# A hybrid decoder block in fp32 on one core: every third low part of the weights, from the 70th tile on, subtracted by GpSimd and not by VectorE

## The chip, the core and the metric

The kernel runs on one core of a Trainium2 chip. A core has TensorE (PE in the profile; its weight loads are PEld), VectorE (DVE), ScalarE (ACT), GpSimd (POOL) and SyncE (SP), each with an instruction queue of its own that is worked off in order, and 16 DMA engines. The metric is the time of one execution of the whole program on the device, in microseconds (us).

## The reference

One decoder block for a sequence of 256 tokens of width 2048, in float32:

```python
mod = jax.nn.silu(c) @ w_ada[l] + b_ada[l]
sh1, sc1, g1, sh2, sc2, g2 = jnp.split(mod, 6, axis=-1)
h = modulate(rms_norm(x, norm1_g[l]), sh1, sc1)
proj = h @ w_in[l]                                  # 2048 -> 6144
...                                                 # attention heads and gated short convolutions
x = x + g1[:, None, :] * (mixed @ w_out[l])         # 2048 -> 2048
h2 = modulate(rms_norm(x, norm2_g[l]), sh2, sc2)
u = causal_dwconv(h2 @ w_ffn_up[l], ffn_conv_w[l], ffn_conv_b[l])   # 2048 -> 11264
u_gate, u_up = jnp.split(u, 2, axis=-1)
ffn = (jax.nn.silu(u_gate) * u_up) @ w_ffn_down[l]  # 5632 -> 2048
x = x + g2[:, None, :] * ffn
```

All weights are read once; there is one sequence, so every weight matrix meets only 256 tokens.

## The kernel before

The matrix products run on TensorE in the type fp32r, and each float32 operand is carried as two fp32r numbers: a high part, the operand rounded to fp32r, and a low part, the operand less its high part. A product is the sum of three: high by high, high by low and low by high.

The weights of the four large products (`w_in`, `w_out`, `w_ffn_up`, `w_ffn_down`) come in 202 pieces, called slots in the code and numbered from 0. A piece holds four blocks (in the last product also three or two) of 128 rows by 512 columns, so it is a tile `raw` of 128 partitions by 2048 elements (1536, 1024). Slots 0 to 47 are `w_in`, 48 to 63 `w_out`. From slot 64 on come the feed-forward layers in four segments, each first through `w_ffn_up` and then through the rows of `w_ffn_down` that belong to it: up 64 to 95, down 96 to 111, up 112 to 131, down 132 to 143, up 144 to 163, down 164 to 175, up 176 to 191, down 192 to 201.

Every piece passes through these steps:

- `load_next` (line 228) issues the piece's DMA on SP's queue (lines 247 and 252) into one of 6 `raw` buffers. The rows of `w_ada`, with which the conditioning vector is multiplied, share this queue and these buffers (line 300).
- `split_hi` (line 260) has ACT round the piece into a tile `hi` (line 266). For two pieces of the last product DVE first multiplies the piece by a gate (line 264).
- `split_lo` (line 269) has DVE subtract `hi` from `raw` into a tile `lo` (line 272). Both inputs lie in SBUF. When this and the rounding are done the `raw` buffer is free, and `load_next` is called for the next transfer.
- The slot's matmuls use `hi` and `lo`: lines 866 (high) and 869 (low) in `w_ffn_up`, line 852 in its first 8 slots, lines 432 (low), 434 and 435 (high) in the other products.

There are 3 buffers each of `hi` and `lo`.

The order of the instructions on every engine is written by hand: the pool is under `manual_schedule`, and the loop of lines 1336 to 1360 walks over the slots. In the turn of slot i it emits the split of slot i + 2, then or before it the small tasks that a table has put there, then the matmuls of slot i, then the work of the `w_ada` tiles that are due in that slot. So a piece's low part is emitted two slots ahead of its use, and a slot takes TensorE 4 to 6 us.

DVE's other work in the feed-forward part: the multiply-adds of `w_ada` (line 330, elements by a column of the conditioning vector, summed in place), the sums of partial products out of PSUM (line 762), the two taps of the convolution (line 730), the product of the gate and up halves (line 781) and its low part (line 784), and the layer's scaled and shifted input `h2` (lines 682 and 687 for two chunks of it, 695 and 707 for others). At the end lines 813, 814 and 811 scale and add the results.

GpSimd has constants and a few small DMAs at the start, and twice the start of a wide `w_ada` sum (`Ada.home`, lines 304 to 310): a memset of 128 by 2048 elements and a DMA of 8 KB on its own queue. Its second pair is emitted at slot 100's split.

Of the kernel before, what the change touches and what calls it, by code (L numbers as in the profile page):

```python
# [8 lines left out]
F32 = mybir.dt.float32  # L9
F32R = mybir.dt.float32r  # L10
AF = mybir.ActivationFunctionType
ALU = mybir.AluOpType
# [16 lines left out]

CFG = {'ada': [[0, 12, 512, False, 17, 4], [4, 8, 512, False, 66, 9], [0, 4, 512, True, 4, 6],
# [102 lines left out]
def tile_block(  # L135
# [5 lines left out]
    nc = tc.nc  # L141
    mm = nc.tensor.matmul
    act = nc.scalar.activation
    V = nc.vector
# [8 lines left out]

    N_T2K, N_T1K, N_RAW, N_HL, N_T4K = CFG["bufs"]

# [72 lines left out]
    def load_next():  # L228
        if pending:
            if isinstance(pending[0], Ada):  # L230

                pending.pop(0).home()
                return
            t = sb.tile([P, 4, 512], F32, tag="raw", bufs=N_RAW, name="raw")
            pending.pop(0)(t)
            ready.append(t)
# [23 lines left out]
    def split_hi(nk, gate=None):  # L260
# [5 lines left out]
        act(hi[:, :nk], t[:, :nk], AF.Copy)  # L266
        halfway.append((t, hi, nk))

    def split_lo():
        t, hi, nk = halfway.pop(0)  # L270
        lo = sb.tile([P, 4, 512], F32R, tag="lo", bufs=N_HL, name="lo")
        V.tensor_tensor(out=lo[:, :nk], in0=t[:, :nk], in1=hi[:, :nk].bitcast(F32), op=ALU.subtract)  # L272
        splits.append((hi, lo))
        load_next()

# [123 lines left out]
    def at(i, f, *a):  # L399
        tasks.setdefault(i, []).append((CFG["cls"].get(f.__name__, 0), f, a))  # L400

# [62 lines left out]
    turns, upto = [], {}  # L464
    for f, ka, kb in CFG["turns"]:
        fs, step = ((f,), 4) if f in COL else ((f + "0", f + "1"), 2)
# [9 lines left out]
    for i, (fs, k) in enumerate(turns):  # L476
        def near(f, d):
            u = uses[f]
            n = u.index(i) + d
            return 0 <= n < len(u) and abs(u[n] - i) <= CFG["keep"].get(f, CFG["near"])  # L480

# [107 lines left out]
    for n, (f, part, k) in enumerate(seq):  # L589
# [7 lines left out]
        if f < 3 and k == 4:  # L597
            at(i + CFG["hold"][f], hold_a, f)
        elif f < 3 and k == 12:
            at(i + CFG["evac"][f], evac_out, f)  # L600
            at(i + CFG["sq"][f], sq_out, f)
# [678 lines left out]
    hi, lo = (sb.tile([P, 4, 512], F32R, tag=g, bufs=N_HL, name=g) for g in ("hi", "lo"))  # L1280
# [26 lines left out]
    xn_copy(6, 7)  # L1307
    split_hi(slots[1][1])
    split_lo()

    vecs = []
# [24 lines left out]
    for i in range(len(slots)):  # L1336
        more = i + LA < len(slots)
        hi_late = i == N_OUT or i in CFG["hi_late"]
        last = i in CFG["x_first"]
        if more and not hi_late and not last:  # L1340
            split_hi(slots[i + LA][1], gated.get(i + LA))
        now[0] = i
        todo = sorted(tasks.pop(i, []), key=lambda e: e[0])
        for c, f, a in todo:
            if c < 2:
                f(*a)
        if more and hi_late and not last:
            split_hi(slots[i + LA][1], gated.get(i + LA))
        if more and not last:
            split_lo()  # L1350
        for c, f, a in todo:
            if c == 2:
                f(*a)
        hi, lo = splits.pop(0)
        slots[i][2](hi, lo)
        for g, r in extra.get(i, []):
            g.consume(r)
        if more and last:
            split_hi(slots[i + LA][1], gated.get(i + LA))
            split_lo()  # L1360
# [33 lines left out]
```

## Time and profile before

| | |
|---|---|
| time, median of 3 runs | 1169.39 us (1168.94 to 1169.49) |
| profiled execution: span from its first to its last instruction | 1167.8 us |
| median of the runs less this span | 1.6 us |
| TensorE's granted clock over the span | 1.000 |
| low parts (line 272) | 201, of them 130 from slot 72 on |
| DMA, mean over the span | 272 GB/s |

The profile is one execution. It states its span and no time of its own beside it; the 1.6 us are what the unprofiled runs take longer than the span of the profiled one, and stand for what lies around the program's instructions. "Idle before" in a row is the time in which the engine did nothing just ahead of the instruction, and the arrow names the work whose end released it. In a view over stretches of time, "busy" is the time in the stretch in which the engine worked. A group's "mean ns" is the mean duration of one instruction.

### The profile page before, as it was taken

Reading aid. Unit: us, or ns where it says so; the run is one execution under the profiler, and the core shown is the slowest. Engines: PE = TensorE matmul, PEld = TensorE weight load, DVE = VectorE, ACT = ScalarE, POOL = GpSimd, SP = SyncE. Lnnn points to the kernel's source line nnn. Section 1 sums busy time; section 2 is a strip of 40 time slices with the busy share of each in tenths; the row PEclk is TensorE's granted clock in tenths of the full one; section 3 lists DMA queues with packets and bytes.
Section 4 is the critical chain, followed back from the end, with each engine's and each line's share of the span. In section 5 each row is a group of like instructions: output and inputs, shape, how many; then the busy total and the mean of one; then the engine's idle time right before and its main releaser. Section 6 shows DMA issues by size and latency. Waiting matters only on the chain.

```text
span 1167.8 us, 15668 instructions
## 1 busy us (share of the span) xinstructions
PE 1150.5 (99%) x6115; PEld 973.7 (83%) x6115; DVE 922.0 (79%) x1030; ACT 625.9 (54%) x906; POOL 12.0 (1%) x24
## 2 busy tenths in 40 slices
PE   5999999999999999999999999999999999999998
PEld 3777778888887889988888888888888888888887
DVE  3889989999999978899976767986655576577767
ACT  5645365567785565566664434455435455335451
POOL 1000000000000000000000000000000000000000
PEclk9999999999999999999999999999999999999999
DMA  9999989999899799974555897984564555675451
GB/s 361 406 415 406 409 323 362 390 346 346 288 346 338 251 319 337 364 258 166 185 202 183 304 342 277 315 290 160 198 227 156 198 181 195 225 247 181 145 180 73
DMA packets 189051, 318.00 MB, mean 272 GB/s; under 512 B 7072, under 2 KB 105844, under 8 KB 184624
## 3 DMA queue, kind: packets, MB, share of 16 engines
q1 hardware_dynamic: 187232, 314.60, 75.5%
q10 hardware_dynamic: 1296, 2.16, 0.5%
q8 instruction: 48, 0.79, 0.3%
q0 software_dynamic: 448, 0.24, 0.1%
q14 instruction: 27, 0.22, 0.0%
HBM read 312.77 MB, written 4.19 MB: 271 GB/s over the span
## 4 chain that ended last, share of the span: by engine, by line
PE 91%; DMA 3%; DVE 3%; ACT 2%; issue 0%; SPq 0%; ACTq 0%
PE z L866 24%; PE z L869 12%; PE z L852 3%; PE ada L324 1%; PE mk L434 1%; PE mk L435 1%; PE mk L432 1%; PE mq L434 1%; DVE lo L272 1%; PE mq L435 1%; PE mq L432 1%; DVE ada L330 1%; PE mc L434 1%; PE mx L434 1%; PE mx L435 1%; PE mc L435 1%
## 5 line engine op out<-in xcount | busy, mean ns | idle before, releaser
L272 DVE TENSOR_TENSOR lo<-raw,hi 128x2048 fp32r<-128x2048 f32 (+2 forms) x201 | 445.9, 2224 | 139.2 <-ACT hi L266 120.7
L266 ACT ACTIVATE hi<-raw 128x2048 fp32r<-128x2048 f32 (+2 forms) x201 | 373.6, 1865 | 311.9 <-PE z L866 58.5
L866 PE MATMUL z<-h,hi 128*128 128x512 f32 x1280 | 299.0, 390 | 0.2 <-DVE h L687 0.2
L866 PEld LDWEIGHTS z<-h,hi 128*128 128x128 f32 x1280 | 237.5, 188 | 48.2 <-PE z L866 0.6
L330 DVE SCALAR_TENSOR_TENSOR ada<-raw,csil,ada 128x512 f32<-128x512 f32 (+3 forms) x167 | 195.4, 1175 | 5.7 <-DMA raw<-in_w_ada_dram 2.2
L869 PEld LDWEIGHTS z<-h,lo 128*128 128x128 f32 x1280 | 159.3, 191 | 3.4
L869 PE MATMUL z<-h,lo 128*128 128x256 f32 x1280 | 160.5, 283 | 0.0
L730 DVE SCALAR_TENSOR_TENSOR uy<-ub,fc,uy 128x254 f32<-128x254 f32 (+1 forms) x176 | 71.3, 476 | 0.2
L762 DVE TENSOR_TENSOR ub<-z,ub 128x256 f32<-128x256 f32 x96 | 33.9, 416 | 37.9 <-ACT ub L759 37.9
L783 ACT ACTIVATE gh<-uy 128x512 fp32r<-128x512 f32 x22 | 13.9, 632 | 63.2 <-DVE uy L781 63.2
L852 PE MATMUL z<-h,hi 128*128 128x256 f32 x256 | 46.6, 284 | 0.4 <-ACT h L684 0.2
L725 ACT ACTIVATE uy<-ub,fc,fc 128x256 f32<-128x256 f32 x88 | 45.6, 602 | 0.0
L759 ACT ACTIVATE ub<-z 128x256 f32<-128x256 f32 x96 | 28.8, 384 | 31.4 <-PE z L866 31.4
L852 PEld LDWEIGHTS z<-h,hi 128*128 128x128 f32 x256 | 40.0, 192 | 0.8 <-ACT h L684 0.5
L852 PE MATMUL z<-h,lo 128*128 128x256 f32 x128 | 36.2, 283 | 0.0
L324 PE MATMUL ada<-raw,crep 128*32 128x256 f32 (+1 forms) x192 | 20.3, 534 | 7.9 <-DMA raw<-in_w_ada_dram 7.9
L784 DVE TENSOR_TENSOR gl<-uy,gh 128x512 fp32r<-128x512 f32 x22 | 15.2, 693 | 15.4 <-ACT gh L783 15.4
L434 PE MATMUL mq<-hi,h 128*128 128x512 f32 x64 | 25.5, 398 | 0.4 <-DVE adaz L361 0.4
L434 PE MATMUL mx<-hi,h 128*128 128x512 f32 x64 | 25.7, 401 | 0.0
L434 PE MATMUL mc<-hi,h 128*128 128x512 f32 x64 | 25.6, 400 | 0.0
L434 PE MATMUL mk<-hi,h 128*128 128x512 f32 x64 | 25.1, 393 | 0.0
L434 PE MATMUL mv<-hi,h 128*128 128x512 f32 x64 | 25.1, 392 | 0.0
(612 smaller groups left out, 1881.2 us busy)
## 6 DMA issues: line engine op xcount, KB each, us to landing
raw<-in_w_ada_dram SPq DMA_DIRECT2D x96, 1024.0 KB, 6.7
raw<-in_w_ffn_up_dram SPq DMA_DIRECT2D x176, 512.0 KB, 4.4
raw<-in_w_in_dram SPq DMA_DIRECT2D x47, 1024.0 KB, 7.6
raw<-in_w_ffn_down_dram SPq DMA_DIRECT2D x28, 1024.0 KB, 5.0
raw<-in_w_out_dram SPq DMA_DIRECT2D x16, 1024.0 KB, 5.4
raw<-in_w_ffn_down_dram SPq DMA_DIRECT2D x20, 768.0 KB, 4.2
xr<-in_x_dram SPq DMA_DIRECT2D x2, 1024.0 KB, 6.7
x<-in_x_dram SPq DMA_DIRECT2D x8, 256.0 KB, 6.9
```

The costliest lines, as they stand in the source:

```text
L266: act(hi[:, :nk], t[:, :nk], AF.Copy)
L272: V.tensor_tensor(out=lo[:, :nk], in0=t[:, :nk], in1=hi[:, :nk].bitcast(F32), op=ALU.subtract)
L324: mm(self.acc[q:q + 32, :], crep[:, i, :], t[:, j, :], start=(r == 0 and j < 4), stop=(r == self.tiles - 1 and j >= self.rows - 4), tile_p ...
L330: V.scalar_tensor_tensor(out=self.acc, in0=t[:, j, :], scalar=csil[:, i:i + 1], in1=self.acc, op0=ALU.mult, op1=ALU.add)
L434: mm(o, a, hi[:, k, s], start=(first and k == 0), stop=False)
L435: mm(o, b, hi[:, k, s], start=False, stop=False)
L725: act(y[:, s], b[:, s], AF.Identity, bias=bias[:, i + j:i + j + 1], scale=w[2][:, i + j:i + j + 1])
L730: V.scalar_tensor_tensor(out=o[:, d:], in0=v[:, :256 - d], scalar=w[2 - d][:, i + j:i + j + 1], in1=o[:, d:], op0=ALU.mult, op1=ALU.add)
L762: V.tensor_tensor(out=d, in0=zp[grp][ft][:, :256], in1=d, op=ALU.add)
L852: mm(o, w[:, j, a], h2T[k + j][:, v * 256:v * 256 + 256], start=begins and j == 0 and w is hi and not v, stop=ends and j == 3 and w is lo)
L866: mm(zp[grp][ft], hi[:, j, ft * P:(ft + 1) * P], h2T[k + j], start=begins and j == 0, stop=ends and j == 3)
L869: mm(zp[grp][ft][:, :256], lo[:, j, ft * P:(ft + 1) * P], h2T[k + j][:, :256], start=False, stop=False)
```

## The change

A counter numbers the calls of `split_lo`. The first call is that of slot 1 (slot 0 is split by hand), so the number is the slot's. From number 70 on, every number that 3 divides has its subtraction issued on GpSimd's queue; all others stay on DVE. Those are slots 72, 75, 78 and so on to 201, 44 pieces in all.

```diff
+CFG = {'other': [70, 3],
...
+    split_no = [0]
+
     def split_lo():
         t, hi, nk = halfway.pop(0)
         lo = sb.tile([P, 4, 512], F32R, tag="lo", bufs=N_HL, name="lo")
-        V.tensor_tensor(out=lo[:, :nk], in0=t[:, :nk], in1=hi[:, :nk].bitcast(F32), op=ALU.subtract)
+        split_no[0] += 1
+        other = split_no[0] >= CFG["other"][0] and split_no[0] % CFG["other"][1] == 0
+        (nc.gpsimd if other else V).tensor_tensor(out=lo[:, :nk], in0=t[:, :nk], in1=hi[:, :nk].bitcast(F32),
+                                                  op=ALU.subtract)
         splits.append((hi, lo))
         load_next()
```

Tiles, sizes, buffers, the order in which the instructions are emitted, and the other engines' work stay as they are.

More of the change, by code (lines that the diff above doesn't have):

```diff
@@ L28 @@
 SH1, SC1, G1, SH2, SC2, G2 = range(6)
-CFG = {'ada': [[0, 12, 512, False, 17, 4], [4, 8, 512, False, 66, 9], [0, 4, 512, True, 4, 6],
+CFG = {'other': [70, 3],
+ 'ada': [[0, 12, 512, False, 17, 4], [4, 8, 512, False, 66, 9], [0, 4, 512, True, 4, 6],
          [4, 0, 1024, False, 23, 22], [0, 8, 512, True, 11, 12], [0, 2, 256, True, 0, 5],
```

## Prediction

> **What bounds the kernel.** I read the page first, then who waited for whom, then the busy time by stretch, then single places in order of time.
>
> ```profile
> PE 1150.5 (99%) x6115; PEld 973.7 (83%) x6115; DVE 922.0 (79%) x1030; ACT 625.9 (54%) x906; POOL 12.0 (1%) x24
> ...
> PE 91%; DMA 3%; DVE 3%; ACT 2%; issue 0%; SPq 0%; ACTq 0%
> ...
> L272 DVE TENSOR_TENSOR lo<-raw,hi 128x2048 fp32r<-128x2048 f32 (+2 forms) x201 | 445.9, 2224 | 139.2 <-ACT hi L266 120.7
> ```
>
> TensorE is busy 99% of the span and is 91% of the chain that ended last. The low parts are DVE's largest group, but DVE has idle time. All waits of PE:
>
> ```profile
> PE ada L324 <- DMA raw<-in_w_ada_dram: 7.9, 3, 7.1
> PE pv_ccol L201 <- DMA vcb<-in_c_dram: 4.6, 1, 4.6
> PE mq L434 <- DVE adaz L361: 0.4, 1, 0.4
> PE mg L496 <- ACT h L1297: 0.4, 1, 0.4
> PE z L852 <- ACT h L684: 0.2, 1, 0.2
> PE z L866 <- DVE h L687: 0.2, 1, 0.2
> ```
>
> Columns: sum, times, longest, in us. The first moved piece, slot 72, is subtracted at 467 us (below). From there on only the last row's 0.2 us is a wait of PE's matmuls. So a faster DVE can win next to nothing, and the change can lose only where a low part, or DVE work behind it, becomes late by more than its slack. Whether there is slack depends on the stretch:
>
> ```profile
> 464.20:488.29 24.09, 24.09 (x175) 22.74 (x174) 23.04 (x24) 12.01 (x23) 0.00 (x0) 1.00 1.05 364
> 505.64:557.55 51.91, 51.91 (x299) 45.88 (x298) 47.20 (x72) 32.77 (x49) 0.00 (x0) 1.00 0.63 213
> 728.80:765.82 37.02, 37.02 (x210) 32.58 (x209) 34.24 (x35) 16.62 (x18) 0.00 (x0) 1.00 0.93 319
> ```
>
> The columns are the stretch, its length, busy time of PE, PEld, DVE, ACT and POOL, then PE's clock, DMA share and GB/s. PE is busy without a gap, and DVE is idle for only 24.09 - 23.04 = 1.05, 51.91 - 47.20 = 4.71 and 37.02 - 34.24 = 2.78 us. These are the places where a disturbance of DVE is felt. The n-th instruction of line 272 belongs to slot n, so slots are found by counting.
>
> **What is removed.** 44 subtractions leave DVE's queue, up to 2.29 us each (2048 elements); issued back to back they advance it by 2.24 (the pair of 4.49 us below). DVE also loses the wait for ACT's `hi` ahead of them. Worth to the end: the 0.2 us above, and as much as 0.3 at the last slot, by the list of who waited for line 272:
>
> ```profile
>   PEld m('D', 3, 3)0_9720 L432: 0.3, 1
> ```
>
> **What is added: the duration.** The trace has no GpSimd instruction with two inputs. The nearest rows:
>
> ```profile
> 174.98 1.82 POOL L308 MEMSET ada<- 128x2048 f32 x1 [79.11 <-DVE ada L330]
> ```
> ```profile
> 172.80 0.75 DVE L328 TENSOR_SCALAR ada<-raw,csil 128x1024 f32<-128x1024 f32 x1
> 173.58 1.29 DVE L330 SCALAR_TENSOR_TENSOR ada<-raw,csil,ada 128x1024 f32<-128x1024 f32 x1
> 174.79 4.49 DVE L272 TENSOR_TENSOR lo<-raw,hi 128x2048 fp32r<-128x2048 f32 x2
> ```
>
> POOL writes 2048 elements per partition in 1.82 us. If it passes the two inputs one after the other at that pace, with the write beside them, a piece costs 3.64; with all three in a row 5.46; the floor is 1.82. I take T = 4.53, half way between 3.64 and 5.46, an estimate. The Trainium skill (GPSIMD Engine Reference, 3.1) gives a measured 4497 ns for this operation at 2048 fp32 elements against 2293 on VectorE; DVE's row agrees (2.29), POOL's no run shows, and by it the sum below would be 0.3 us smaller.
>
> **What is added: the effect on DVE.** The decisive unknown is whether POOL can read two inputs while DVE reads two. Bounds: side by side costs DVE nothing, and strict turns cost it T for each piece, less the 2.24 it no longer spends. In the rows above the memset lies beside the pair of subtractions, which are not stretched, so a POOL write disturbs nothing; that is no reading. Two rows lean to turns. DVE passes 1024 elements in 0.75 us with one input (line 328) and in 1.29 with two (line 330): a one-input operation gets the second read path's help, so a two-input operation fills both. And once a POOL instruction that reads lies beside a DVE one:
>
> ```profile
> 1.01 0.29 POOL masks.py:199 TENSOR_SCALAR_AFFINE_SELECT ident<-ident 128x128 f32<-128x128 f32 x1
> ```
> ```profile
> 1.03 0.35 DVE L188 CAST onesr<-ones 128x128 fp32r<-128x128 f32 x1
> 1.93 0.23 DVE L194 CAST maskb<-mask 128x128 bf16<-128x128 f32 x1 [0.54 <-POOL mask L191]
> ```
>
> That cast took 0.35 us against 0.23 for a cast of the same size later, to another type: weak, but on the same side. I take turns, so a moved piece costs DVE 4.53 - 2.24 = 2.29 us more than before. A page speaks against this change outright: the Trainium skill (SBUF — State Buffer, Who interferes with whom) says that a VectorE instruction with two SBUF inputs contends with a GpSimd instruction that reads SBUF, and that whichever comes second is blocked until the first is done. No run here shows it; by it the sum is the one that I take, without it the first rival's.
>
> Nearly all of DVE's work here has two SBUF inputs (lines 330, 730, 781, 784, 767 and the remaining 272); line 762, out of PSUM, has one and passes. Now the places.
>
> **Place 1, slot 76.**
>
> ```profile
> 467.07 2.29 DVE L272 TENSOR_TENSOR lo<-raw,hi 128x2048 fp32r<-128x2048 f32 x1 [0.58 <-ACT hi L266]
> ...
> 486.08 2.29 DVE L272 TENSOR_TENSOR lo<-raw,hi 128x2048 fp32r<-128x2048 f32 x1
> 488.29 1.41 DVE L762 TENSOR_TENSOR ub<-z,ub 128x256 f32<-128x256 f32 x4
> ...
> 499.46 0.48 DVE L687 SCALAR_TENSOR_TENSOR h<-h2f,B,h 128x256 fp32r<-128x256 f32 x1 [0.18 <-ACT h L684]
> ```
> ```profile
> 500.09 3.89 PE L866 MATMUL z<-h,hi 128*128 128x512 f32 x16 [0.18 <-DVE h L687]
> ```
>
> The first two rows are slots 72 and 75. PE at 500.09 waits for the `h2` of line 687, which comes at the end of a chain of DVE and ACT steps that begins at 488.29. No slack: two moved pieces are 4.58 late, less the 1.05 idle of the stretch, 3.5 us.
>
> **Place 2, slot 87.**
>
> ```profile
> 557.55 2.29 DVE L272 TENSOR_TENSOR lo<-raw,hi 128x2048 fp32r<-128x2048 f32 x1
> ```
> ```profile
> 559.16 4.01 PEld L869 LDWEIGHTS z<-h,lo 128*128 128x128 f32 x32
> ```
>
> The 32 loads are the last 16 of slot 86 and the first 16 of slot 87 (a slot that ends a sum begins with its low products, line 863), which thus needs its low part at 559.16 + 2.0 = 561.2; it had it at 559.84, slack 1.3. Of DVE's 4.71 us idle since 505.64, 2.1 are three waits for ACT between lines 781 and 784 that move along with the work:
>
> ```profile
> L784 DVE TENSOR_TENSOR gl<-uy,gh 128x512 fp32r<-128x512 f32 x3 | 2.1, 692 | 2.1 <-ACT gh L783 2.1
> ```
>
> 2.6 can be filled. Slots 78, 81 and 84 make DVE 3 x 2.29 = 6.9 late, less 2.6, 4.3; ACT's `hi` of slot 87 stands behind that same chain. Its own subtraction is 4.53 - 2.29 = 2.2 longer: 4.3 + 2.2 - 1.3 = 5.2 us.
>
> **Place 3, slot 125.**
>
> ```profile
> 765.82 2.29 DVE L272 TENSOR_TENSOR lo<-raw,hi 128x2048 fp32r<-128x2048 f32 x1
> ```
> ```profile
> 768.45 4.01 PEld L869 LDWEIGHTS z<-h,lo 128*128 128x128 f32 x32
> ```
>
> Needed at 768.45 + 2.0 = 770.45, there at 768.11: slack 2.3. Since 728.80 DVE's idle time consists of hand-backs from ACT that move along, and slots 120 and 123 make it 4.6 late: 2.3 us.
>
> **Place 4, the last slot, 201.**
>
> ```profile
> 1153.65 2.28 DVE L264 TENSOR_TENSOR raw<-raw,ada 128x2048 f32<-128x2048 f32 x1
> 1158.00 2.29 DVE L272 TENSOR_TENSOR lo<-raw,hi 128x2048 fp32r<-128x2048 f32 x1 [2.06 <-ACT hi L266]
> ```
> ```profile
> 1160.34 0.98 PE L432 MATMUL m('D', 3, 3)0_9720<-lo,gh 128*128 128x512 f32 x3
> ```
>
> PE uses this low part the moment it is there, so 2.2 us more are 2.2 us later, unless the gate multiplication at 1153.65 moves ahead: two moved pieces before it (195, 198) leave DVE, 4 us at most. Between 0 and 2.2; I take 1.0.
>
> Elsewhere I find no slot whose slack is used up by the moved pieces since DVE's last gap, and count nothing. Queues: POOL has only these subtractions, and one memset and DMA after slot 100's split, which wait for that slot's work on DVE and for no moved piece; the next moved piece is two slots later. On SP the load that takes a moved piece's `raw` buffer waits up to 2.2 us longer (4.5 under turns), and the transfers queued behind it wait too.
>
> **The sum.** 3.5 + 5.2 + 2.3 + 1.0 = 12.0 on the profiled span of 1167.8 makes 1179.8; the median of the runs is 1.6 above that span: 1181.4 us. With T = 3.64 a piece costs 1.40 more: 2.8 - 1.05 = 1.75; 4.2 - 2.6 + 1.35 - 1.3 = 1.65; 2.8 - 2.3 = 0.5; end 0: 3.9, so 1173.3. With T = 5.46 (3.22 more): 5.4; 9.7 - 2.6 + 3.2 - 1.3 = 9.0; 4.1; end 2: 20.5, so 1189.9.
>
> **Rivals.** *Side by side* (the other side: not slower). POOL reads while DVE reads, and no place pays. DVE is 2.24 earlier for each piece ahead of slots 76, 87 and 125; slot 87's 4.53 - 2.29 - 1.3 = 0.9 is covered by slot 84's departure, and slot 201 by those of 195 and 198. Time 1169.4, at best 0.5 less. It decides as soon as a piece takes less than about 2.8 us from DVE: then place 1's 2 x (2.8 - 2.24) is within its 1.05 of idle time. For it: the unstretched pair beside the memset. Against: the two rows above. *Starved*: DVE keeps its reads as long as it has work, and POOL waits for a gap. From 469.36, where slot 72's subtraction ended, to 486.08 there is next to none, so it would run from 486.08 to 490.6, and slot 72 needs it here:
>
> ```profile
> 480.22 2.08 PE L869 MATMUL z<-h,lo 128*128 128x256 f32 x16
> ```
>
> That is 10.4 us late, three times place 1; with half that excess at the other places about twice the sum, 1193. For it: nothing in the trace; against: an engine that gets each turn at the end of an instruction needs no gap. *Faster*: only from those 0.5 us and a shorter tail.
>
> **Chances.** Turns 0.58, of which 0.02 end within 0.2% (2.3 us, about what a measurement of this kernel can tell from no change); starved 0.08; side by side 0.31, of which 0.28 are within 0.2% and 0.03 slower, where T is at its upper end and the last slot pays; faster 0.03. So slower 0.56 + 0.08 + 0.03 = 0.67, same 0.30, faster 0.03. The likeliest case's own range is 1173 to 1190; since side by side holds 0.31 the range reaches to it: 1168.8 to 1190.
>
> **What would show it.** Right: POOL busy some 190 us in 44 instructions of line 277; DVE two-input instructions of unchanged shape that last longer, or stand idle with POOL as releaser or with none, while POOL runs; PE waits at lines 687, 869 and 432 of 2 to 5 us near 500, 561 and 770 us. Wrong: the remaining DVE subtractions keep 2.29 us with POOL running beside them and PE has no wait, or a POOL piece lasts beyond 5.5 us with DVE undisturbed.

## The result and the profile after

| | before | after |
|---|---|---|
| time, median (range) | 1169.16 us (1168.93 to 1169.49) | 1181.21 us (1180.29 to 1182.67), 4 runs |
| profiled execution: span | 1167.8 us | 1178.5 us (that run's own time 1180.29 us) |
| ratio of the times, 95% interval | | 1.0103 [1.0091, 1.0116] |

The change costs 12.05 us; the forecast was 1181.4 us. In the program after, `split_lo` is line 277; every line of before behind it has its old number plus 6 (330 is 336, 687 is 693, 866 is 872).

First the engines and the chain that ended last, from the page of after:

```profile
PE 1152.1 (98%) x6115; PEld 974.6 (83%) x6115; DVE 923.5 (78%) x986; ACT 625.1 (53%) x906; POOL 219.1 (19%) x68
...
PE 86%; DVE 5%; DMA 3%; issue 3%; ACT 2%; POOLq 0%; POOL 0%; SPq 0%; ACTq 0%; DVEq 0%
```

DVE has 44 instructions fewer, 986 for 1030, and is busy 1.5 us longer than before. GpSimd has 207 us more. TensorE does the same 6115 matmuls, and its share of the chain falls from 91% to 86%; DVE gains 2 points and "issue", time for which the profile shows no releaser, 3. The groups of after show where DVE's relief went:

```profile
L277 DVE TENSOR_TENSOR lo<-raw,hi 128x2048 fp32r<-128x2048 f32 (+2 forms) x157 | 363.0, 2316 | 142.6 <-ACT hi L267 136.7
L277 POOL TENSOR_TENSOR lo<-raw,hi 128x2048 fp32r<-128x2048 f32 (+1 forms) x44 | 207.1, 4706 | 782.2 <-ACT hi L267 760.5
...
L336 DVE SCALAR_TENSOR_TENSOR ada<-raw,csil,ada 128x512 f32<-128x512 f32 (+3 forms) x167 | 212.8, 1279 | 5.7 <-DMA raw<-in_w_ada_dram 2.1
...
L736 DVE SCALAR_TENSOR_TENSOR uy<-ub,fc,uy 128x254 f32<-128x254 f32 (+1 forms) x176 | 105.9, 672 | 3.8 <-ACT uy L731 3.8
L768 DVE TENSOR_TENSOR ub<-z,ub 128x256 f32<-128x256 f32 x96 | 34.0, 416 | 37.1 <-ACT ub L765 37.1
```

DVE's low parts fall by 445.9 - 363.0 = 82.9 us. The multiply-adds of `w_ada` and the convolution's taps are the same instructions of the same shapes as before, where they read

```profile
L330 DVE SCALAR_TENSOR_TENSOR ada<-raw,csil,ada 128x512 f32<-128x512 f32 (+3 forms) x167 | 195.4, 1175 | 5.7 <-DMA raw<-in_w_ada_dram 2.2
L730 DVE SCALAR_TENSOR_TENSOR uy<-ub,fc,uy 128x254 f32<-128x254 f32 (+1 forms) x176 | 71.3, 476 | 0.2
```

and take 17.4 and 34.6 us more. Line 768 is as it was (33.9 us, 416 ns each, at line 762 before): its first input lies in PSUM. So the instructions with two inputs in SBUF were stretched, and a stretched instruction counts as busy. What TensorE waited for, after:

```profile
PE adac L365 <- DVE adaz L383: 3.4, 1, 3.4
PE z L875 <- POOL lo L277: 3.0, 1, 3.0
PE z L875 <- DVE lo L277: 1.8, 1, 1.8
PE m('D', 3, 3)0_9720 L438 <- POOL lo L277: 0.8, 1, 0.8
```

Four waits are new, one for each place of the prediction, 9.0 us together; the span is 10.7 us longer. The first, after, on DVE, on GpSimd and on TensorE:

```profile
465.82 10.49 DVE L336 SCALAR_TENSOR_TENSOR ada<-raw,csil,ada 128x512 f32<-128x512 f32 x8
...
483.66 7.45 DVE L336 SCALAR_TENSOR_TENSOR ada<-raw,csil,ada 128x512 f32<-128x512 f32 x4
491.02 0.15 DVE L383 SCALAR_TENSOR_TENSOR adaz<-adaz,vbc 128x4 f32<-128x4 f32 x1
```
```profile
466.54 4.62 POOL L277 TENSOR_TENSOR lo<-raw,hi 128x2048 fp32r<-128x2048 f32 x1 [289.54 <-ACT hi L267]
483.09 5.10 POOL L277 TENSOR_TENSOR lo<-raw,hi 128x2048 fp32r<-128x2048 f32 x1 [11.94 <-ACT hi L267]
```
```profile
491.25 0.63 PE L365 MATMUL adac<-ident,ada 128*128 128x128 f32 x4 [3.37 <-DVE adaz L383]
```

Before, the same eight multiply-adds, and TensorE's transposes of the finished `w_ada` sum (line 365 after), stood so:

```profile
469.28 6.13 DVE L330 SCALAR_TENSOR_TENSOR ada<-raw,csil,ada 128x512 f32<-128x512 f32 x8
```
```profile
488.14 0.60 PE L359 MATMUL adac<-ident,ada 128*128 128x128 f32 x4
```

The eight took 6.13 us and now take 10.49. The 4.36 us more are one GpSimd subtraction, which began beside them at 466.54. The four at 483.66, 3.11 us before, are drawn out in the same way by slot 75's piece. The third place is the wait at line 875 for a low part on DVE. The second, after:

```profile
567.57 3.35 PE L875 MATMUL z<-h,lo 128*128 128x256 f32 x16 [2.95 <-POOL lo L277]
```
```profile
568.13:571.54 3.41, 3.41 (x16) 3.25 (x15) 3.34 (x3) 0.03 (x1) 0.00 (x0) 0.50 0.81 273
```

The second row is a stretch right behind that wait, with the columns that the prediction explains: for 3.41 us TensorE's granted clock is 0.50. Sixteen low matmuls of this shape took 2.08 us at 480.22 before (slot 72); these 16 take 3.35.

### The profile page after: what moved, and what is told of

Same layout as the page of the kernel before. It is cut to its first block, busy times and chain, and to the rows that moved or that the text cites. A ratio compares the mean times of both kernels' runs of the same rounds, so it can differ in the third digit from the quotient of the medians.

```text
span 1178.5 us, 15676 instructions
## 1 busy us (share of the span) xinstructions
PE 1152.1 (98%) x6115; PEld 974.6 (83%) x6115; DVE 923.5 (78%) x986; ACT 625.1 (53%) x906; POOL 219.1 (19%) x68
## 4 chain that ended last, share of the span: by engine, by line
PE 86%; DVE 5%; DMA 3%; issue 3%; ACT 2%; POOLq 0%; POOL 0%; SPq 0%; ACTq 0%; DVEq 0%
PE z L872 21%; PE z L875 11%; PE z L858 4%; DVE ada L336 2%; DMA raw<-in_w_ada_dram 2%; DVE lo L277 2%; PE mk L440 1%; PE mk L441 1%; PE mk L438 1%; PE ada L330 1%; PE mq L440 1%; PE mq L441 1%; PE mq L438 1%; PE mx L440 1%; PE mc L440 1%
## 5 line engine op out<-in xcount | busy, mean ns | idle before, releaser
L277 DVE TENSOR_TENSOR lo<-raw,hi 128x2048 fp32r<-128x2048 f32 (+2 forms) x157 | 363.0, 2316 | 142.6 <-ACT hi L267 136.7
L277 POOL TENSOR_TENSOR lo<-raw,hi 128x2048 fp32r<-128x2048 f32 (+1 forms) x44 | 207.1, 4706 | 782.2 <-ACT hi L267 760.5
L336 DVE SCALAR_TENSOR_TENSOR ada<-raw,csil,ada 128x512 f32<-128x512 f32 (+3 forms) x167 | 212.8, 1279 | 5.7 <-DMA raw<-in_w_ada_dram 2.1
L736 DVE SCALAR_TENSOR_TENSOR uy<-ub,fc,uy 128x254 f32<-128x254 f32 (+1 forms) x176 | 105.9, 672 | 3.8 <-ACT uy L731 3.8
L790 DVE TENSOR_TENSOR gl<-uy,gh 128x512 fp32r<-128x512 f32 x22 | 26.9, 1223 | 15.9 <-ACT gh L789 15.9
L783 ACT ACTIVATE uy<-uy 128x512 f32<-128x512 f32 x22 | 13.8, 625 | 23.2 <-DVE uy L736 23.1
```

The lines of the kernel that those rows point to most:

```text
L277: (nc.gpsimd if other else V).tensor_tensor(out=lo[:, :nk], in0=t[:, :nk], in1=hi[:, :nk].bitcast(F32), op=ALU.subtract)
L336: V.scalar_tensor_tensor(out=self.acc, in0=t[:, j, :], scalar=csil[:, i:i + 1], in1=self.acc, op0=ALU.mult, op1=ALU.add)
L736: V.scalar_tensor_tensor(out=o[:, d:], in0=v[:, :256 - d], scalar=w[2 - d][:, i + j:i + j + 1], in1=o[:, d:], op0=ALU.mult, op1=ALU.add)
```

## The experiments

The theory: DVE and GpSimd take turns where both read SBUF, so a moved piece gives DVE no relief and costs it about 2.3 us; this is paid where TensorE needs DVE's work without slack, at the four places. The rivals: GpSimd is merely slow and only the pieces themselves come late (side by side); GpSimd starves beside a busy DVE; the price is spread over all 44 pieces.

### The disputed cost by itself: side_by_side

The whole block is left out and the output is zeros. DVE and GpSimd run independent instructions on tiles of their own, alone and beside each other, with a meeting of the engines between stretches:

```python
v_two(4); meet(); g_two(4); meet()   # alone
v_two(8);  g_two(4); meet()          # DVE 2048 elements, two SBUF inputs
v_short(24); g_two(4); meet()        # DVE 512 elements
v_psum(24);  g_two(4); meet()        # DVE: one input in PSUM
v_one(12);   g_two(4); meet()        # DVE: one SBUF input (tensor_scalar)
v_two(8);  g_one(4); meet()          # GpSimd: a copy, one input
v_two(8);  g_none(8); meet()         # GpSimd: memset, no input
s_one(8);  g_two(4); meet()          # ACT: one input
g_one(3); meet(); v_one(4); meet()   # one input, alone
```

> This kernel leaves the whole block out and writes zeros; it sets streams of instructions beside each other, stretch by stretch, with a meeting of the engines between. Alone: 4 VectorE subtractions of 2048 elements with two SBUF inputs, then 4 on GpSimd. Beside 4 GpSimd subtractions: 8 VectorE subtractions of 2048; 24 of 512; 24 of 512 with one input in PSUM; 12 multiplications of 2048 with one SBUF input; 8 ScalarE copies. Beside 8 VectorE subtractions: 4 GpSimd copies (one input) and 8 GpSimd memsets (none). Theory of turns: alone 2.29 and 4.5 us each; 8 VectorE and 4 GpSimd subtractions together take the sum, 8 x 2.24 + 4 x 4.5 = 36 us, with single VectorE rows of 2.3 + 4.5 us and others of 2.29; the PSUM rows keep 0.68 us and the memsets and ScalarE disturb nothing and are not disturbed. Rival, a shared rate: all rows in the stretch grow alike, VectorE's to 3 to 4 us, together 24 to 30 us. Rival, no contention: the longer of the two streams, 18 us, and VectorE's rows stay at 2.29. What the one-input operations do, neither theory says beforehand: if a one-input VectorE operation borrows the second read path it waits as the two-input ones do.

Measured; the stretches are in the order of the code, and some are left out:

```profile
L76 DVE TENSOR_TENSOR vo<-va,vb 128x2048 f32<-128x2048 f32 x4 | 9.2, 2292 | 0.6 <-DMA vb<-in_x_dram 0.5
L92 POOL TENSOR_TENSOR go<-ga,gb 128x2048 f32<-128x2048 f32 x4 | 18.0, 4493 | 0.3
...
L76 DVE TENSOR_TENSOR vo<-va,vb 128x2048 f32<-128x2048 f32 x8 | 35.1, 4382 | 0.2
L92 POOL TENSOR_TENSOR go<-ga,gb 128x2048 f32<-128x2048 f32 x4 | 23.8, 5939 | 0.2
...
L92 POOL TENSOR_TENSOR go<-ga,gb 128x2048 f32<-128x2048 f32 x4 | 18.0, 4510 | 0.2
L84 DVE TENSOR_TENSOR vo<-pb,vb 128x512 f32<-128x512 f32 x24 | 16.6, 690 | 0.8
...
L76 DVE TENSOR_TENSOR vo<-va,vb 128x2048 f32<-128x2048 f32 x8 | 24.6, 3078 | 0.2
L96 POOL COPY go<-ga 128x2048 f32<-128x2048 f32 x4 | 13.4, 3349 | 0.2
L76 DVE TENSOR_TENSOR vo<-va,vb 128x2048 f32<-128x2048 f32 x8 | 18.3, 2291 | 0.2
L100 POOL MEMSET go<- 128x2048 f32 x8 | 14.4, 1805 | 0.4
```

Alone a subtraction of 2048 elements takes 2.29 us on DVE and 4.49 on GpSimd. Together, 8 and 4 of them take DVE 35.1 us, and one after the other they would take 8 x 2.29 + 4 x 4.49 = 36.3: turns. With an input in PSUM (690 ns) and beside a memset (2291 ns) DVE is undisturbed; beside a copy (1.89 us alone) it is not. The Trainium skill (SBUF — State Buffer, "Who interferes with whom") has the same division: two SBUF inputs on VectorE against a GpSimd instruction that reads SBUF, and whoever comes second waits. The trace agrees in each of these rows.

How the turns are dealt out shows in the stretch with short DVE instructions, at the start of it:

```profile
73.18 14.69 DVE L80 TENSOR_TENSOR vo<-va,vb 128x512 f32<-128x512 f32 x3
```
```profile
73.02 14.29 POOL L92 TENSOR_TENSOR go<-ga,gb 128x2048 f32<-128x2048 f32 x3
```

In 14.7 us DVE gets three instructions done that last 0.69 us alone, against three of GpSimd: one for one. Each is recorded at 4.9 us, its wait included. An engine that gets its turn at the end of each instruction of the other does not starve; the rival of that name is out.

### Only the disturbance: extra_read and extra_write

DVE keeps all its subtractions. At the 44 places GpSimd reads, or only writes, a tile of its own that nobody uses. Room for it comes from two buffers fewer of one tile, in both.

```diff
+    spare = const.tile([P, 2048], F32, name="spare")
...
+        if other:
+            nc.gpsimd.tensor_copy(spare[:, :1], hi[:, 0, :1].bitcast(F32))
+            nc.gpsimd.tensor_tensor(out=spare, in0=spare, in1=spare, op=ALU.subtract)
+        V.tensor_tensor(out=lo[:, :nk], in0=t[:, :nk], in1=hi[:, :nk].bitcast(F32), op=ALU.subtract)
```

extra_write has two `nc.gpsimd.memset(spare, 0.0)` in place of the subtraction of `spare`.

> VectorE keeps all low parts as in the kernel before. At the 44 moved places GpSimd subtracts a spare tile from itself as soon as the piece's high part is there (a copy of one element ahead of it waits for that), and nobody waits for the result; no raw buffer is read. Theory of turns: each costs VectorE its whole 4.5 us and not 2.3, so place 1 pays 2 x 4.5 - 1.1 = 8 us, place 2 about 3 x 4.5 - 2.6 - 1.3 = 10, place 3 about 7, the end up to 4, and slots that were spared come in: 1195 to 1205 us. Rival, only the moved pieces' own length counts: 1169.4, since no moved piece is late. Rival, buffers that come free late: 1169.4, too. Rival, a shared rate at which both slow down by half: 1175 to 1185.

> As the run before, with two memsets of the spare tile (3.6 us of GpSimd, no input) in place of the subtraction. Theory of turns, which is one of reads: 1169.4 within 0.5 us and VectorE's rows unstretched. Rival, any GpSimd instruction that touches SBUF keeps VectorE out: 3.6 in place of 4.5 us each, about 1190.

Measured: extra_read 1200.01 us, ratio 1.0265 [1.0248, 1.0282]; extra_write 1169.19 us, ratio 1.0001 [0.9992, 1.001]. The engines of extra_read, and its group of added reads:

```profile
PE 1159.7 (97%) x6115; PEld 978.3 (82%) x6115; DVE 1031.0 (86%) x1030; ACT 625.0 (52%) x906; POOL 269.3 (22%) x113
```
```profile
L281 POOL TENSOR_TENSOR spare<-spare 128x2048 f32<-128x2048 f32 x44 | 192.0, 4363 | 3.5
```

DVE does exactly the work of before and is busy 109 us longer, 2.5 for each read, and gives up no subtraction against it; so it costs more than the change itself (part of its 30.9 us is a lower granted clock, 0.992). In extra_write GpSimd is at work nearly as long, DVE is only 2.4 us busier than before (924.4), and the time is the same:

```profile
L282 POOL MEMSET spare<- 128x2048 f32 x88 | 159.6, 1813 | 5.1
```

So it is the reading. Side by side is out: in extra_read GpSimd computes no tensor that TensorE waits for, and reads no `raw` buffer, and it is the slowest of all versions of the block here.

### What the relief is worth by itself: relief

```diff
+        if other:
+            nc.gpsimd.memset(lo[:, :nk].bitcast(F32), 0.0)
+        else:
+            V.tensor_tensor(out=lo[:, :nk], in0=t[:, :nk], in1=hi[:, :nk].bitcast(F32), op=ALU.subtract)
```

> At the 44 moved places no low part is computed: GpSimd fills the tile with zeros (a memset, which reads nothing), so that part of the products is left out. VectorE is relieved of 44 x 2.24 us with no GpSimd reading beside it. What the change could have won at most: by the waits of PE in the kernel before, 0.2 us at slot 76 and 0.3 at slot 201, so 1168.6 to 1169.3. Rival, a bound on VectorE that the waits do not show: several us less, 1165 or below.

Measured: 1168.79 us, ratio 0.9999 [0.999, 1.0008]. Its engines:

```profile
PE 1150.2 (99%) x6115; PEld 974.0 (83%) x6115; DVE 828.8 (71%) x986; ACT 626.6 (54%) x906; POOL 89.1 (8%) x68
```

DVE is relieved of 93 us at once, disturbed by nothing, and the time is the same. What the change could have won was nothing to begin with, as TensorE's 0.2 us of waiting for DVE had it.

### Where it is paid: nine and other35

Nine slots lie at or ahead of the four places; the other 35 are the rest.

```diff
-        other = split_no[0] >= CFG["other"][0] and split_no[0] % CFG["other"][1] == 0
+        other = split_no[0] in (72, 75, 78, 81, 84, 87, 120, 123, 201)
```

other35 moves exactly those of the 44 that this list leaves out.

> Only the nine moved pieces of the prediction's places stay on GpSimd: slots 72, 75, 78, 81, 84, 87, 120, 123 and 201. Theory of turns at few places: nearly the whole loss, 1179 to 1182 us (the last slot pays up to 2.2 and not 0.9, since 195 and 198 are back on VectorE). Rival, a loss in proportion to the moved pieces: 9/44 of 12 us, 1171.7. Rival, only the moved pieces' own length: slots 87 and 201 alone pay, 0.9 + 2.2, 1172.3.

> The complement: 35 moved pieces stay on GpSimd, the nine of the prediction's places are back on VectorE. Theory of turns at few places: 1169.0 to 1170.0, although 35 x 4.6 us of GpSimd work block VectorE as before; VectorE's rows are stretched, and PE has no new wait. Rival, a loss in proportion: 35/44 of 12, 1178.7.

Measured: nine 1183.52 us, ratio 1.0124 [1.0109, 1.0139]; other35 1169.38 us, ratio 1.0002 [0.9993, 1.0011]. What TensorE waited for that is new, in nine:

```profile
PE adac L365 <- DVE adaz L383: 3.4, 1, 3.4
PE z L875 <- POOL lo L277: 2.9, 1, 2.9
PE m('D', 3, 3)0_9720 L438 <- POOL lo L277: 2.2, 1, 2.2
PE z L875 <- DVE lo L277: 1.8, 1, 1.8
```

The nine have the whole cost. The other 35 cost DVE its turns too (its time in their program falls by 922.0 - 905.0 = 17 us only, where 35 x 2.24 = 78 were taken from it), and no wait of TensorE comes of it. A price spread over the pieces is out. The last slot pays 2.2 us in nine and 0.8 in after: without slots 195 and 198 moved, the gate multiplication does not come earlier. Nine was 1.5 us over the upper end of what was expected, its profiled run (1182.88 us) 0.9. The clock accounts for that much; the same stretch in nine and in after:

```profile
492.30 6.16 PE L872 MATMUL z<-h,hi 128*128 128x512 f32 x16
```
```profile
491.64 3.89 PE L872 MATMUL z<-h,hi 128*128 128x512 f32 x16
```

Behind the same wait of 3.4 us the same 16 matmuls run slow in nine and at full speed in after, and TensorE loses 5.9 us at this place against 3.7. At the second place it is the other way round, 3.1 against 4.7. The two runs of nine above 1184 us have a lower clock still (0.996 against 0.997 over the span).

### The places one by one: first_two, before_87 and two_lone

The list of slots in the diff above becomes (72, 75), (78, 81, 84) and (87, 201).

> Only slots 72 and 75 on GpSimd. Theory of turns: place 1 alone, 3.5 us, paid as one wait of PE of 3.2 to 3.5 us near 488 us at the transposes that read the finished w_ada sum, and none at slot 76: 1172.7. Rival, only the pieces' own length: both have over 5 us of slack and nobody waits, 1169.4.

> Only slots 78, 81 and 84 on GpSimd; slot 87 is back on VectorE. Theory of turns: VectorE comes 4.3 us late to slot 87, whose slack is 1.3: a wait of PE of 3.0 us there, 1172.4, and up to 1.5 more if the granted clock falls after the wait as it did in the changed kernel, 1173.9. Rival, only the pieces' own length: their slack is 5 us or more, 1169.4.

> Only slots 87 and 201 on GpSimd, each without moved pieces ahead of it. By the sum: slot 87 waits 2.2 + 0.1 - 1.3 = 1.0 us (its GpSimd subtraction takes 4.6, not 2.29), slot 201 waits 2.3 us, since 195 and 198 are on VectorE and the gate multiplication is not advanced; 1172.7. If moving 195 and 198 off VectorE did nothing for the end, slot 201 waits 0.8 to 0.9 as in the changed kernel: 1171.3. If VectorE's stretch alone made the loss: 1169.4.

| | measured, us | ratio | more than before |
|---|---|---|---|
| first_two | 1174.48 (1173.92 to 1175.04) | 1.0042 [1.0027, 1.0058] | 5.2 |
| before_87 | 1170.11 (1169.91 to 1170.29) | 1.0006 [0.9997, 1.0015] | 0.8 |
| two_lone | 1173.96 (1172.30 to 1174.09) | 1.0035 [1.0022, 1.0047] | 4.6 |

The waits and the clock of first_two, the stretch being the one behind its wait:

```profile
PE adac L365 <- DVE adaz L383: 3.4, 1, 3.4
```
```profile
491.00:498.00 7.00, 6.87 (x20) 5.61 (x21) 3.91 (x12) 4.66 (x15) 0.00 (x0) 0.56 1.05 375
```

The wait is the one of after, and TensorE runs at half its clock for about 6.2 of these 7 us (a mean of 0.56). The profiled run, 1175.01 us, is 5.7 above before: 3.4 of waiting and some 2.3 of slow clock. In two_lone the runs fall into two kinds by themselves: granted clock 1.000 over the span, 1172.30 and 1172.65 us; 0.998, 1173.96, 1174.06 and 1174.09. The first kind is 3.0 to 3.3 above before, which is what the two waits say (they are those of the profiled run, one of the second kind, whose clock fell to half for 3.41 us at 1164.10, behind the wait of 2.2):

```profile
PE m('D', 3, 3)0_9720 L438 <- POOL lo L277: 2.2, 1, 2.2
PE z L875 <- POOL lo L277: 0.8, 1, 0.8
```

In before_87 the three pieces alone cost less than was expected of them:

```profile
PE z L875 <- DVE lo L277: 0.7, 1, 0.7
```

Its clock stays at 1.00, and its 0.8 us are this wait.

## Why the prediction came out right, and where it did not

**TensorE sets the end, and relief of DVE is worth nothing.** Right: relief takes 93 us from DVE and wins none. No kernel here is faster than the one before.

**The duration.** T was estimated at 4.53 us, half way between two guesses (exactly half way is 4.55). It is 4.49 alone, so the middle was lucky; 4.62 and 5.10 in the two pieces above; and 4.89 in the mean of the 38 full pieces, because some wait for a turn of DVE's (4.71 over all 44, six of which have 1536 elements).

**Turns.** Right, on an argument that was thin (a cast of 0.35 us against 0.23, and two-input operations at half the pace). side_by_side shows it directly, and extra_read against extra_write shows that it is the reading. Of the signs named ahead, POOL's busy time came out as 207 us and not some 190, since the waits for turns count in it.

**Place 1: 3.5 us.** Measured 3.1 at the transposes, 3.7 with the 0.6 us by which this execution was ahead of before's when it came to slot 64. The size is right, the instruction is not: the prediction followed the chain from 488.29 to line 687, but the finished `w_ada` sum leaves DVE just ahead of that chain, and TensorE's transposes of it stand in its queue at 488.14. That sum left DVE at 485.87 before and at 491.11 after, 5.2 later, as only one of the two moved subtractions lies ahead of it to give time back; 2.1 of this was slack. The transposes pay first; at line 693 TensorE and the chain are late by the same, and nothing is left to pay. The expectation of first_two was short by the clock's share.

**Place 2: 5.2 us. This is the step that failed.** It said that slots 78, 81 and 84 make slot 87 4.3 us late. before_87 shows that they make its low part 2.2 us late. The prediction's stretch of 51.91 us, in which DVE was busy for 47.20, reads there

```profile
505.31:559.45 54.14, 54.14 (x311) 47.80 (x310) 50.80 (x69) 32.78 (x49) 14.49 (x3) 1.00 0.63 204
```

DVE is busy 3.6 us longer, where the prediction has 3 x 2.29 = 6.9, and idle 1.4 less, where it fills 2.6. The price of a piece was set too high. These are the rows that the three pieces stretched:

```profile
506.08 5.04 DVE L277 TENSOR_TENSOR lo<-raw,hi 128x2048 fp32r<-128x2048 f32 x1 [0.67 <-ACT hi L267]
...
516.43 7.60 DVE L736 SCALAR_TENSOR_TENSOR uy<-ub,fc,uy 128x255 f32<-128x255 f32 x8
...
537.94 4.34 DVE L790 TENSOR_TENSOR gl<-uy,gh 128x512 fp32r<-128x512 f32 x1 [0.70 <-ACT gh L789]
```

Before they took 2.29, 3.24 and 0.69, so the turns cost 2.8, 4.4 and 3.7 us and not 4.53 each, 10.8 together in place of 13.6, which is most of the difference. The first piece began on GpSimd at 504.33, beside sums out of PSUM (line 768) that were not stretched and then DVE's own wait of 0.67 for ACT; only what was left of it blocked DVE. The third lay in part beside the wait of 0.70. TensorE then waits 0.7 for the three alone, 0.8 for slot 87's own longer subtraction alone, and 3.0 for all together, as the slack of 1.3 is used up once: 2.2 + 2.2 - 1.3 = 3.1. The total came near all the same, 4.7, because the halved clock behind that wait added some 1.6 us, which the prediction did not have. Two errors of opposite sign: that this place came out near is luck.

**Places 3 and 4: 2.3 and 1.0.** Measured 2.0 and 0.9 of lateness. That 195 and 198 bring the gate multiplication forward is shown by nine, in which they stay and the last slot pays 2.2.

**Elsewhere nothing.** Right: other35.

**The sum.** 3.7 + 4.7 + 2.0 + 0.9 = 11.3, less the 0.6 that after was ahead at the start, is 10.7, the difference of the spans (1178.5 - 1167.8). Without the clock's 1.6 it would be 9.1, which is the four waits, 9.0. That the median came within 0.2 us of the forecast is partly luck: the runs of after lie between 1180.29 (clock 0.999) and 1182.67 (0.996).

## What to carry to other kernels

GpSimd is no spare VectorE for operations that read SBUF: while it reads, a two-input instruction of DVE waits until GpSimd's is done, so a piece moved away comes back as stretch. Where DVE had no gap this was twice what was given up, 4.36 us for 2.24. Before moving work off an engine, ask which wait of the bounding engine that engine ends: here it was 0.2 us, and that is the most there was to win, whatever DVE's busy share. And price a moved piece by what lies beside it: work out of PSUM or a wait of DVE's own took up part of its time, so that a turn cost 2.8 to 4.4 us.

## What the runs showed of the hardware that was not expected

- **Turns are one for one, whatever their lengths.** Of DVE's 24 instructions of 512 elements beside four subtractions on GpSimd, only those that met one were touched, but each of these paid in full, 4.9 us for 0.69. Short instructions suffer most: the 128x254 taps rose from 476 to 672 ns in the mean.
- **Busy time hides the waiting.** A blocked instruction is recorded as running, so neither DVE's busy time (923.5 us against 922.0) nor a wait of DVE's names the culprit; what gives it away is the same shape with a longer duration.
- **One SBUF input alone is no protection.** Beside GpSimd's subtractions a DVE `tensor_scalar` of 2048 elements was blocked as well, in the stretch with 12 of them:

```profile
L88 DVE TENSOR_SCALAR vo<-va,one 128x2048 f32<-128x2048 f32 x12 | 31.9, 2658 | 0.4
```

It takes 1.28 us alone, so four turns of about 4.1 us are in the 31.9. A rounding on ACT beside the same subtractions kept its 1.91 us.
- **Whether a wait halves TensorE's clock depends on where it falls.** In every trace here the moments at which the granted clock changes lie whole multiples of 3.413 us apart. Cut into stretches at such moments, the waits of the first and second place look so, in after and then in nine (behind the bounds stand the length and TensorE's busy time; TensorE's clock is the third number from the end):

```profile
486.21:489.62 3.41, 1.67 (x8) 1.05 (x6) 3.34 (x3) 1.21 (x4) 1.98 (x1) 1.00 1.08 379
564.72:568.13 3.41, 0.56 (x4) 0.56 (x5) 3.41 (x4) 1.55 (x1) 2.80 (x1) 1.00 0.00 0
```
```profile
486.90:490.31 3.41, 1.29 (x6) 0.75 (x4) 3.34 (x3) 1.21 (x4) 1.60 (x1) 1.00 1.09 383
565.41:568.82 3.41, 1.66 (x14) 1.45 (x13) 2.74 (x5) 3.25 (x6) 3.41 (x1) 1.00 0.00 0
```

In after the first wait is cut into two parts and nothing happens; nearly all of the second falls into one stretch, and at its end, 568.13, the clock is halved. In nine it is the other way round, and the clock is halved at 490.31. Over all stretches of the ten traces of the block, at full clock, each in which TensorE was busy for 1.60 us or less was followed by half the clock, and none with 1.65 or more was. So the length of a wait does not decide: the 2.2 us at the last slot did it in two_lone (1.21 busy) and not in nine (1.65). A stretch at half the clock that TensorE filled gave the full clock back; one that the wait still reached into (up to 2.81 busy) did not. So the clock stayed down for 3.41 or 6.83 us, at a price of some 1.6 us at the second place of after and 2.1 to 2.3 at the first of nine and first_two. The Trainium skill (TensorE: Matmul & The Clock Gate, "What's actually happening") describes a free-running window of 3413 ns in which TensorE's activity is judged. The traces agree in the length, and in that the same wait halves the clock in one execution and not in another.
